# Up projection by seven products for eight, output projection by quarters of tokens, up results by way of DRAM

## The chip, the cores and the metric

One core of a Trainium2 chip runs the whole program. Its engines are TensorE (PE, with its weight loads PEld), VectorE (DVE), ScalarE (ACT), GpSimd (POOL) and SyncE (SP), from whose queue all DMAs of this kernel go out. The metric is the device time of one execution in microseconds, as the median of several runs.

## The reference

One inference step of a hybrid decoder layer in float32, for 1024 prompt tokens and 8 x 4 sample tokens (T = 1056 tokens in all), 1024 features. The part around the change:

```
hn  = rms_norm(x, norm_mix_pre)
mix = hybrid_mixer(hn, ...)        # three head groups, concatenated, then mix @ w_out  (1024 x 1024)
x   = x + rms_norm(mix, norm_mix_post)
hn  = rms_norm(x, norm_ffn_pre)
up  = hn @ w_up                    # 1024 x 5632: gate | val, 2816 features each
gate = causal_dwconv(gate)         # width 3; new state is an output
f   = (gelu(gate) * val) @ w_down  # 2816 x 1024
y   = x + rms_norm(f, norm_ffn_post)
```

## The kernel before

Activations lie with features on the 128 partitions and tokens along the free dimension. A product in float32 is made of three fp32r matmuls: each operand is split into a rounded part and the rest (`wh` and `wl` for weights, `xh` and `xl` for tokens), and `wh xh + wh xl + wl xh` is summed in one PSUM bank. `load_w` (L256) brings a weight tile of 128 outputs, up to 8 k of 128 x 128 (512 KB), by one DMA into the staging tile `w` (one buffer), casts it to `wh` on ACT (L264) and subtracts on POOL to `wl` (L265); `wh` and `wl` have two buffers each. `dense` (L268) runs the 3 x 8 matmuls of one output tile for one group of G = 352 tokens (three groups).

The order of PE's instructions in the mixer and the output projection is written out by `Weave` (L116): streams of work with ranks, each step yielding how long its next step has to wait by a virtual clock; what can't go yet is filled with dense work. Near its end the small products of the sample tokens (`samples`) are woven with the output projection. `project` (L1567) runs output tiles for groups 0 and 1 while the samples go on, then the rest and group 2, with further weight tiles and staging tiles (`places`, `stage`) cut out of memory that the mixer no longer needs. `finish` (L1620) normalises a group, adds the input, writes the sum to DRAM (`x1_dram`), and splits the next operands (L330). The factor per token of the second norm is not applied to the operands but to each product when it leaves PSUM (`scaled`, L296).

The ConvFFN (from L1655) goes through 22 tiles of hidden features in five parts. `gate_conv` (L1663) makes the gate tile for three groups, the convolution on ACT and DVE (L1682) and the gelu; `value` (L1687) the other tile, the product of both (L1695 to L1698), and its split into `hidh` and `hidl` (L1700, L1701), which stay in SBUF. After each part `down` (L1705) multiplies its hidden tiles with 8 output tiles of the down weights for three groups and adds into `fa` on DVE (L1734). In the last part `final` (L1746) of one group is laid between the products of the next; its steps are the sum of squares (L344), `rstd_of` (L305), two element-wise passes (L1754, L1755) and the output DMAs.

Of the kernel before, what the change touches and what calls it, by code (L numbers as in the profile page):

```python
# [8 lines left out]
F32 = mybir.dt.float32  # L9
# [14 lines left out]
KD = D // P  # L24
G = 352
NG = 3
NCH = SEQ // P
# [4 lines left out]
QUARTERS = ((0, 5), (5, 10), (10, 14), (14, 18), (18, 22))  # L32
# [3 lines left out]
# (kind, unit, tiles as (section, tile in the section, conv tile or None))  # L36
# [6 lines left out]
# the order of the dense work of the mixer  # L43
# [3 lines left out]
# columns of the packed vectors  # L47
# [9 lines left out]
# how far the urgent steps go ahead in the scheduler's order  # L57
FIRST = 1500
# how far apart two steps of one stream are set in the tensor engine's order, by what comes between them
# [5 lines left out]
    s_norm=6310, rows1=9000, rows2=6960, rows3=8500, f_rows=18400, f_0=5120, f_1=8920,  # L65
# [4 lines left out]
CUT = 4  # L70
# [8 lines left out]
LAST = 3  # L79

# columns of the packed constants
# [12 lines left out]
def constants():  # L94
# [5 lines left out]
    # what takes the place of NEG and LV for the samples  # L100
# [92 lines left out]
def kernel(ctx: ExitStack, tc: tile.TileContext, I, O):  # L193
# [31 lines left out]
    hnp = ctx.enter_context(tc.tile_pool(name="hnp", bufs=1))  # L225
    wp = ctx.enter_context(tc.tile_pool(name="wp", bufs=2))
    left, right = ExitStack(), ExitStack()
# [22 lines left out]
    x1_dram = drp.tile([NG, P, KD, G], F32, name="x1_dram")  # L250
# [32 lines left out]
    def hn_operand(k, g):  # L283
        return hh[g][:, k, :], hl[g][:, k, :]
# [1596 lines left out]
```

## Time and profile before

| | us |
|---|---|
| runs | 1575.71, 1578.13, 1581.62 (median 1578.13) |
| span of the profiled execution | 1578.6 |
| PE busy in it | 1496.2 |
| DVE busy | 920.7 |
| ACT busy | 542.1 |
| POOL busy | 546.1 |
| mean granted clock of PE | 0.977 |

The profiled execution has its span, from the first to the last instruction, and no other time of its own. A busy share is the union of an engine's instructions; matmuls are pipelined, so that one lasts longer than its distance from the next. The page cuts the span into slices; the views below cut it into stages: up to 652 us the mixer, then the samples with the output projection, the seam to the ConvFFN, the ConvFFN from 814.7 on, and what comes after its last product at 1558.2.

### The profile page before, as it was taken

The numbers are of one execution on the slowest core, as the hardware profiler recorded it, in microseconds if no ns is written. First come the engines' busy times: TensorE is split into PE (matmuls) and PEld (weight loads), VectorE is DVE, ScalarE is ACT, GpSimd is POOL, SyncE is SP. The second block draws the span as 40 slices with busy tenths as digits, with TensorE's granted clock in tenths as the row PEclk, the third lists the DMA queues.
The fourth block names the chain that finished last, engine by engine and source line by source line (L and its number), as shares of the span: only waits on it lengthen the run. The fifth ranks groups of instructions, "written<-read, shape, count | busy, mean of one in ns | idle before, by whom it ended". The sixth has DMA issues, their size and how long they took to land.

```text
span 1578.6 us, 24157 instructions
## 1 busy us (share of the span) xinstructions
PE 1496.2 (95%) x9438; PEld 1453.1 (92%) x9438; DVE 920.7 (58%) x1818; ACT 542.1 (34%) x1173; POOL 546.1 (35%) x624
## 2 busy tenths in 40 slices
PE   8788999989999999999899999999999999999995
PEld 8788899879989989988889999999999999999994
DVE  6889888796474367636975522444245325424558
ACT  7644445443342232424652211221122112212353
POOL 6234433232354353566432122221222222122224
PEclk9989999999999999999999999999999999999997
DMA  5111010111111231324531112111111111111142
GB/s 180 43 48 30 23 45 25 34 32 30 43 55 47 79 112 47 102 76 152 187 100 41 44 42 62 41 41 42 52 54 34 41 61 42 40 55 54 52 151 110
DMA packets 51210, 100.63 MB, mean 64 GB/s; under 512 B 14857, under 2 KB 25737, under 8 KB 50713
## 3 DMA queue, kind: packets, MB, share of 16 engines
q1 hardware_dynamic: 51096, 99.10, 20.1%
q8 instruction: 74, 1.21, 0.3%
q14 instruction: 40, 0.32, 0.1%
HBM read 85.25 MB, written 13.31 MB: 62 GB/s over the span
## 4 chain that ended last, share of the span: by engine, by line
PE 63%; DVE 17%; ACT 6%; POOL 5%; issue 4%; DMA 4%; SPq 0%; DVEq 0%; POOLq 0%; ACTq 0%
PE acc L203 55%; PE mc L203 3%; PE mb L203 3%; DVE kq L465 2%; PE mb L207 2%; DMA E<-rows_dram 2%; POOL wl L265 1%; DVE hl L333 1%; DVE two L784 1%; DVE v L465 1%; ACT sq L212 1%; POOL E L868 1%; PE po L203 1%; DVE fs L344 1%; ACT E L212 1%
## 5 line engine op out<-in xcount | busy, mean ns | idle before, releaser
L203 PE MATMUL acc<-hh,wh 128*128 128x352 f32 x1952 | 660.7, 339 | 18.2 <-DVE pre L303 12.2
L203 PE MATMUL acc<-hh,wl 128*128 128x352 f32 x1960 | 635.8, 324 | 2.6 <-POOL wl L265 2.0
L203 PE MATMUL acc<-hl,wh 128*128 128x352 f32 x1952 | 631.9, 324 | 0.7 <-DVE hl L333 0.7
L203 PEld LDWEIGHTS acc<-hh,wh 128*128 128x128 f32 x1952 | 371.7, 191 | 25.3 <-DVE pre L303 8.5
L265 POOL TENSOR_TENSOR wl<-w,wh 128x1024 fp32r<-128x1024 f32 (+2 forms) x117 | 252.9, 2162 | 362.3 <-ACT wh L264 354.8
L203 PEld LDWEIGHTS acc<-hh,wl 128*128 128x128 f32 x1960 | 372.4, 190 | 4.2 <-POOL wl L265 2.3
L203 PEld LDWEIGHTS acc<-hl,wh 128*128 128x128 f32 x1952 | 373.0, 191 | 3.1 <-DVE hl L333 1.7
L264 ACT CAST wh<-w 128x1024 fp32r<-128x1024 f32 (+2 forms) x117 | 109.9, 939 | 416.4 <-PE acc L203 400.3
L203 PE MATMUL acc<-hidh,wh 128*128 128x352 f32 x444 | 143.8, 324 | 0.0
L203 PE MATMUL acc<-hidh,wl 128*128 128x352 f32 x444 | 143.3, 323 | 0.0
L203 PE MATMUL acc<-hidl,wh 128*128 128x352 f32 x444 | 143.2, 322 | 0.0
L303 DVE TENSOR_TENSOR fpre<-acc,rs 128x352 f32<-128x352 f32 (+1 forms) x88 | 35.8, 430 | 137.5 <-PE acc L203 135.1
L1734 DVE TENSOR_TENSOR fa<-fa,acc 128x352 f32<-128x352 f32 x96 | 49.8, 519 | 106.3 <-PE acc L203 105.9
L1682 DVE SCALAR_TENSOR_TENSOR fy<-fpre,vec,fy 128x1072 f32<-128x1072 f32 x44 | 79.3, 1802 | 36.7 <-ACT fy L212 36.0
L203 PEld LDWEIGHTS acc<-hidh,wh 128*128 128x128 f32 x444 | 83.4, 188 | 0.0
L203 PEld LDWEIGHTS acc<-hidl,wh 128*128 128x128 f32 x444 | 83.4, 188 | 0.0
L203 PEld LDWEIGHTS acc<-hidh,wl 128*128 128x128 f32 x444 | 83.4, 188 | 0.0
L1701 DVE TENSOR_TENSOR hidl<-hid,hidh 128x352 fp32r<-128x352 f32 x66 | 52.7, 799 | 37.8 <-ACT hidh L1700 37.8
L1677 POOL COPY ffn_o<-fpre 128x2 f32<-128x2 f32 x22 | 4.1, 186 | 157.8 <-DVE fpre L303 157.8
L465 DVE SCALAR_TENSOR_TENSOR kq<-pre,cw,kq 128x352 f32<-128x352 f32 (+1 forms) x72 | 53.4, 748 | 7.7 <-ACT kq L212 7.2
L1700 ACT CAST hidh<-hid 128x352 fp32r<-128x352 f32 x66 | 31.9, 483 | 74.2 <-DVE hid L1695 49.9
L303 DVE TENSOR_TENSOR hid<-acc,rs 128x352 f32<-128x352 f32 x66 | 34.4, 521 | 38.1 <-PE acc L203 38.1
(552 smaller groups left out, 2238.7 us busy)
## 6 DMA issues: line engine op xcount, KB each, us to landing
w<-in_w_up_dram SPq DMA_DIRECT2D x44, 512.0 KB
w<-in_w_in_dram SPq DMA_DIRECT2D x30, 512.0 KB
E<-rows_dram SPq DMA_DIRECT2D x24, 256.0 KB
w<-in_w_dn_dram SPq DMA_DIRECT2D x21, 256.0 KB
w<-in_w_out_dram SPq DMA_DIRECT2D x10, 512.0 KB
w<-in_w_dn_dram SPq DMA_DIRECT2D x16, 320.0 KB
xr<-in_xT_dram SPq DMA_DIRECT2D x24, 176.0 KB
hh<-x_dram SPq DMA_DIRECT2D x3, 1408.0 KB
```

Source lines behind the costliest of these rows:

```text
L203: return nc.tensor.matmul(out, **kw)
L207: return nc.tensor.transpose(out, in_, identity)
L212: i = nc.scalar.activation(**kw)
L264: nc.scalar.copy(out=wh[:, ks], in_=w[:, ks])
L265: gtt(out=wl[:, ks], in0=w[:, ks], in1=wh[:, ks].bitcast(F32), op=ALU.subtract)
L303: vtt(out=out, in0=ps, in1=r, op=ALU.mult)
L333: stt(out=hl[g][:, k, :], in0=x, scalar=col(vcol + k), in1=hh[g][:, k, :].bitcast(F32), op0=ALU.mult, op1=ALU.subtract)
L465: stt(out=y[:, a:b], in0=pre[:, a + j:b + j], scalar=cw2[:, 4 * t + j:4 * t + j + 1], in1=y[:, a:b], op0=ALU.mult, op1=ALU.add)
L1682: stt(out=y[:, :LF], in0=pre[:, j:j + LF], scalar=col(V_FW + 3 * f + j), in1=y[:, :LF], op0=ALU.mult, op1=ALU.add)
L1700: nc.scalar.copy(out=hidh[:, groups[g]], in_=hid)
L1701: vtt(out=hidl[:, groups[g]], in0=hid, in1=hidh[:, groups[g]].bitcast(F32), op=ALU.subtract)
L1734: vtt(out=fa[:, g, m, :], in0=fa[:, g, m, :], in1=ps[:, :G], op=ALU.add)
```

## The change

Tokens are now also cut into four quarters of Q = 264.

*Up projection.* Output tiles are taken in pairs, features in two halves of 4 k, tokens in two units of two quarters. Each pair and unit is thus a 2 x 2 by 2 x 2 block product, done by Winograd's form of Strassen's method: seven block products of 4 k x 3 matmuls with 264 columns in place of eight. The combinations of tokens (`operands`) are made once per unit, those of weights (`weight_pieces`) once per pair and use, each then split into two parts. The seven products accumulate in three PSUM banks per unit; between products, DVE or ACT reads a bank, and the next product goes on summing into it. For this the operands must be normalised completely, so `finish` applies the second factor itself.

*Output projection.* Quarters 0 and 1 together, then 2, then 3, each with all 8 weight tiles loaded anew; the subtraction for odd tiles is on DVE. The places and stages set aside are gone. After quarter 3, `head` runs the first pair's gate products for unit 0.

*Up results.* The product of gelu and value goes in float32 to `hid_dram`, and is loaded, cast and subtracted again in the down projection, which now comes as a whole after the up projection, in six parts and by quarters. PE's written order now holds to the program's end; the mixed values are one tile instead of eight.

```diff
+Q = 264
+NQ = 4
+PLACES = ({6: 4, 5: 5, 7: 6, 4: 7, 1: 0, 2: 1, 3: 2}, {1: 3, 6: 8, 5: 9, 7: 10, 2: 11, 4: 12, 3: 13})
+HEAD = 1
-QUARTERS = ((0, 5), (5, 10), (10, 14), (14, 18), (18, 22))
+PARTS = ((0, 2), (2, 6), (6, 10), (10, 14), (14, 18), (18, 22))
...
-            gtt(out=wl[:, ks], in0=w[:, ks], in1=wh[:, ks].bitcast(F32), op=ALU.subtract)
+            tt(out=wl[:, ks], in0=w[:, ks], in1=wh[:, ks].bitcast(F32), op=ALU.subtract)
...
+        def product(m, w, q):
+            ps = yield from dense(accp, w, hn_operand, KS, q, Q)
+            act(out=mix[m][:, quarters[q]], in_=ps[:, :Q], func=AF.Copy, scale=col(V_NPOST + m))
+            act(out=sqs[q][:, m, :], in_=ps[:, :Q], func=AF.Square)
+        def project(qs):
...
+            for m in range(KD):
+                w = load_w(I["w_out"][m], KD, tt=vtt if m % 2 else gtt)
+                for q in qs:
+                    yield from product(m, w, q)
+            for q in qs:
+                xs[q] = on.tile([P, KD, Q], F32, name="x", bufs=2)
+                dma(out=xs[q], in_=I["xQ"][q])
+                weave.add(finish(q, WAIT["f_wait"]), 8)
+        def project_first():
+            yield from project((0, 1))
+            split_mix(2, 0)
+            yield from project((2,))
+            have.add("three")
+        def project_last():
+            split_mix(3, 2)
+            yield lambda: late
+            late.pop(0)()
+            yield from project((3,))
+            have.add("projected")
...
+        def finish(q, wait):
+            t = total(q)
+            yield wait
+            r = rstd_of(on.tile([P, Q], F32, name="rstd", bufs=2), [t])
+            x = xs[q]
+            for i in range(2):
+                ks = slice(KH * i, KH * i + KH)
+                m = mx[:, ks, quarters[q]]
+                vtt(out=m, in0=m, in1=bc(r, 1, KH), op=ALU.mult)
+                vtt(out=x[:, ks], in0=x[:, ks], in1=m, op=ALU.add)
+                act(out=sqs[q][:, ks], in_=x[:, ks], func=AF.Square)
+                dma(out=x1_dram[q, :, ks], in_=x[:, ks])
+            t = total(q)
+            for k in range(KD):
+                act(out=mix[k][:, quarters[q]], in_=x[:, k, :], func=AF.Copy, scale=col(V_FPRE + k))
+            yield WAIT["f_rows"]
+            r = rstd_of(on.tile([P, Q], F32, name="rstd", bufs=2), [t])
...
+            vtt(out=t1, in0=B[0][1], in1=B[0][0], op=ALU.subtract)
+            vtt(out=t2, in0=B[1][1], in1=t1, op=ALU.subtract)
+            split(6, t2)
+            split(5, t1)
+            vtt(out=B[0][1], in0=B[1][1], in1=B[0][1], op=ALU.subtract)
+            split(7, B[0][1])
+            vtt(out=t2, in0=B[1][0], in1=t2, op=ALU.subtract)
+            split(4, t2)
+            late.append(lambda: (split(1, B[0][0]), split(2, B[1][0], gtt)))
+            late.append(lambda: split(3, B[1][1], gtt))
...
+    QS = [(1, 0), (6, 1), (5, 2), (7, 1), (2, 0), (4, 1), (3, 2)]
...
+        def weight_pieces(srcs):
+            A = [[None, None], [None, None]]
+            w = wp.tile([P, KD, P], F32, name="w", bufs=1)
+            for i, j in ((0, 0), (1, 0), (1, 1), (0, 1)):
+                A[i][j] = w[:, KH * i:KH * i + KH] if j == 0 else fg.tile([P, KH, P], F32, name="wq", bufs=2)
+                dma(out=A[i][j], in_=srcs[i][:, KH * j:KH * j + KH])
...
+            yield weight_piece(A[0][0])
+            vtt(out=s1, in0=A[1][0], in1=A[1][1], op=ALU.add)
+            vtt(out=s2, in0=s1, in1=A[0][0], op=ALU.subtract)
+            yield weight_piece(s2)
+            yield weight_piece(s1)
+            vtt(out=A[1][0], in0=A[0][0], in1=A[1][0], op=ALU.subtract)
+            yield weight_piece(A[1][0])
+            yield weight_piece(A[0][1])
+            yield weight_piece(A[1][1])
+            vtt(out=s2, in0=A[0][1], in1=s2, op=ALU.subtract)
+            yield weight_piece(s2)
+        def fast(srcs, units, out):
+            banks, sb = {}, {}
+            for (p, b), (wh, wl) in zip(QS, weight_pieces(srcs)):
+                for u in units:
+                    first = p in (1, 6, 5)
...
+                    for k in range(KH):
+                        kw = dict(skip_group_check=not first)
+                        mm(ps, lhsT=wh[:, k, :], rhs=xh[:, k, :], start=first and k == 0, stop=False, **kw)
+                        mm(ps, lhsT=wh[:, k, :], rhs=xl[:, k, :], start=False, stop=False, **kw)
+                        mm(ps, lhsT=wl[:, k, :], rhs=xh[:, k, :], start=False, stop=k == KH - 1, **kw)
+                        yield 0
+                    if p == 1:
+                        sb[u, 1] = fg.tile([P, Q], F32, name="f1", bufs=2)
+                        nc.scalar.copy(out=sb[u, 1], in_=ps)
+                    elif p in (6, 7):
+                        sb[u, p] = fg.tile([P, Q], F32, name=f"f{p}", bufs=2 if p == 6 else 1)
+                        vtt(out=sb[u, p], in0=sb[u, 1], in1=ps, op=ALU.add)
+                        if p == 7:
+                            out(1, 1, u, sb[u, 7], banks[u, 2])
+                    elif p == 2:
+                        out(0, 0, u, None, ps)
+                    elif p == 4:
+                        out(1, 0, u, sb[u, 1], ps)
+                    elif p == 3:
+                        out(0, 1, u, sb[u, 6], ps)
...
+        def head():
+            yield lambda: "projected" in have
+            late.pop(0)()
+            for i in range(HEAD):
+                pres[i] = gate_pres()
+                yield from fast(w_pair(i, 0), (0,), gate_out(pres[i]))
...
+        gates(0)
+        for i in range(NF // 2):
+            if i + 1 < NF // 2:
+                gates(i + 1)
+            hids = [hid4[:, (2 * i + j) % 4, :] for j in range(2)]
+            drain(fast(w_pair(i, 1), range(2), value_out(ys.pop(i), hids)))
+            for j in range(2):
+                dma(out=hid_dram[2 * i + j], in_=hids[j])
...
+        for qi, (f0, f1) in enumerate(PARTS):
+            hid = []
+            for f in range(f0, f1):
+                x = fp.tile([P, T], F32, name="hx", bufs=2)
+                dma(out=x, in_=hid_dram[f])
+                h, l = (fp.tile([P, T], F32R, name=f"hid{y}{f - f0}", bufs=2) for y in "hl")
+                nc.scalar.copy(out=h, in_=x)
+                vtt(out=l, in0=x, in1=h.bitcast(F32), op=ALU.subtract)
+                hid.append((h, l))
```

## Rows read from the trace of the kernel before

**Rows 1.** The page's first part: busy us, share of the span, instructions of each engine.
```profile
PE 1496.2 (95%) x9438; PEld 1453.1 (92%) x9438; DVE 920.7 (58%) x1818; ACT 542.1 (34%) x1173; POOL 546.1 (35%) x624
```
**Rows 2.** Table by stretches: length, busy us of PE, PEld, DVE, ACT, POOL, clock, DMA.
```profile
652.00:706.00 54.00, 53.32 (x366) 47.42 (x367) 16.30 (x44) 16.45 (x40) 33.55 (x33) 1.00 0.22 77
706.00:760.00 54.00, 53.59 (x305) 48.66 (x304) 38.79 (x46) 26.42 (x52) 35.38 (x20) 1.00 0.50 159
760.00:814.70 54.70, 45.27 (x236) 41.98 (x235) 47.69 (x79) 32.34 (x67) 20.10 (x16) 0.91 0.47 148
814.70:1509.40 694.70, 694.69 (x4346) 694.69 (x4347) 296.27 (x444) 149.92 (x190) 165.38 (x164) 1.00 0.16 51
1509.40:1558.20 48.80, 47.73 (x292) 46.72 (x290) 33.34 (x57) 28.78 (x55) 17.45 (x14) 1.00 0.26 99
1558.20:1578.60 20.40, 2.71 (x4) 1.12 (x4) 16.08 (x24) 3.22 (x6) 9.54 (x9) 0.56 0.37 141
```
**Rows 3.** Chain of waits in order of time: start us, us, what; its longest piece.
```profile
814.71 694.66 PE acc L203 x4344
```
**Rows 4.** Timeline and groups by shape, PE and PEld: matmuls and weight loads of other sizes.
```profile
138.12 0.61 PE L203 MATMUL mb<-V,Gt 128*128 128x128 f32 x4
561.23 1.03 PE L203 MATMUL mb<-qm,kq 128*128 128x256 f32 x4
683.97 0.57 PEld L203 LDWEIGHTS mc<-kqG,hh 128*128 128x128 f32 x4
...
L203 PE MATMUL mb<-V,Gt 128*128 128x128 f32 x128 | 19.0, 275 | 0.0
L203 PE MATMUL mb<-qm,kq 128*128 128x256 f32 x32 | 8.3, 382 | 0.5 <-POOL qm L1088 0.5
L203 PEld LDWEIGHTS mc<-kqG,hh x32: 187/192/192, 681.8 to 691.1; 128*128 128x128 f32 x32
```
**Rows 5.** DMA issues of the output weights: out<-in, count, KB each.
```profile
w<-in_w_out_dram SPq DMA_DIRECT2D x10, 512.0 KB
...
v<-in_w_out_dram SPq DMA_DIRECT2D x5, 512.0 KB
```
**Rows 6.** Chain of waits, the seam: a step on DVE, a weight load's DMA.
```profile
768.25 0.43 DVE mix L1630
...
793.99 3.57 DMA w<-in_w_up_dram
```
**Rows 7.** Instructions on the tile `w`: duration ns min/median/max, first and last start.
```profile
L264 ACT CAST wh<-w x117: 603/1048/1068, 34.8 to 1521.7; 128x1024 fp32r<-128x1024 f32 x83, 128x512 fp32r<-128x512 f32 x18, 128x640 fp32r<-128x640 f32 x16
L265 POOL TENSOR_TENSOR wl<-w,wh x117: 1287/2389/3278, 36.5 to 1522.7; 128x1024 fp32r<-128x1024 f32 x83, 128x512 fp32r<-128x512 f32 x18, 128x640 fp32r<-128x640 f32 x16
...
L265 POOL TENSOR_TENSOR hl<-w,hl x2: 1288/1294/1301, 1509.9 to 1515.5; 128x512 fp32r<-128x512 f32 x2
```
**Rows 8.** Table by stretches of the instructions on `acc` alone (PE, PEld, DVE, ACT).
```profile
652.00:706.00 54.00, 36.82 (x165) 25.84 (x165) 0.00 (x0) 2.71 (x6) 1.00 0.22 77
...
814.70:1509.40 694.70, 694.69 (x4346) 694.69 (x4347) 119.08 (x249) 0.00 (x0) 1.00 0.16 51
1509.40:1558.20 48.80, 47.14 (x288) 46.10 (x286) 11.81 (x23) 0.00 (x0) 1.00 0.26 99
```
**Rows 9.** The page's costliest groups: a convolution step, count | busy, mean ns | idle before.
```profile
L1682 DVE SCALAR_TENSOR_TENSOR fy<-fpre,vec,fy 128x1072 f32<-128x1072 f32 x44 | 79.3, 1802 | 36.7 <-ACT fy L212 36.0
```
**Rows 10.** Instructions on the tile `acc`: an eviction on DVE, ns min/median/max.
```profile
L1734 DVE TENSOR_TENSOR fa<-fa,acc x96: 506/521/522, 1087.9 to 1563.4; 128x352 f32<-128x352 f32 x96
```
**Rows 11.** Timeline of the seam: two additions on DVE, and POOL at that time.
```profile
755.16 0.51 DVE L1630 TENSOR_TENSOR mix<-mix,xr 128x352 f32<-128x352 f32 x1
758.27 2.72 DVE L1630 TENSOR_TENSOR mix<-mix,xr 128x352 f32<-128x352 f32 x1
...
758.10 2.52 POOL L265 TENSOR_TENSOR wl<-v,wh 128x1024 fp32r<-128x1024 f32 x1
```
**Rows 12.** Chain of waits in the tail: the sums over the partitions.
```profile
1563.50 2.73 PE po L203 x4
```

More of the change, by code (lines that the diff above doesn't have):

```diff
@@ L1639 @@
-        on = right.enter_context(tc.tile_pool(name="on", bufs=1, side="right"))
-        ssum = [sums(on, f"ss{g}") for g in range(NG)]
-        with tc.tile_pool(name="smp", bufs=1) as smp:
-            samples(smp)
-            split_mix(0)
-            split_mix(1)
-            weave.add(project(smp), 9)
-            weave.run(lambda: "projected" in have)
-        order.close()
-        weave.run(lambda: not weave.streams)
-        drain(finish(2))
-    right.close()
+                xh, xl = hn_operand(k, q)
@@ new lines, in finish @@
+        def finish(q, wait):
[15 more added lines that the diff above has]
+            r = rstd_of(on.tile([P, Q], F32, name="rstd", bufs=2), [t])
+            if q >= 2:
+                yield lambda: "fx" in have
+            for i in range(2):
+                m = mx[:, KH * i:KH * i + KH, quarters[q]]
+                o = m if q < 2 else xnb[0][:, KH * i:KH * i + KH, Q * (q - 2):Q * (q - 1)]
+                vtt(out=o, in0=m, in1=bc(r, 1, KH), op=ALU.mult)
+            have.add(("normed", q))
+            if q == 1:
+                yield lambda: "fx" in have
+                operands(0, mx)
@@ L1651 @@
+        late = []
+        on = right.enter_context(tc.tile_pool(name="on", bufs=1, side="right"))
+        smp_done = lambda: all(x + " samples" in have for x in ("gdn", "ml", "ssd"))
+        with tc.tile_pool(name="smp", bufs=1) as smp:
+            log_tables()
+            samples(smp)
+            split_mix(0, 0)
+            split_mix(1, 2)
+            weave.add(project_first(), 9)
+            weave.run(lambda: "three" in have and smp_done())
     left.close()
+    LF = 1072
+    QS = [(1, 0), (6, 1), (5, 2), (7, 1), (2, 0), (4, 1), (3, 2)]
@@ new lines, with gates @@
+        fo = ph.enter_context(tc.tile_pool(name="fo", bufs=1, side="right"))
+        fpool[1] = fo
+        operands(1, xnb[0])
+        ffn_o = fo.tile([P, NF, 18], F32, name="ffn_o")
+        st_ffn = fo.tile([P, NF, 16], F32, name="st_ffn")
+        dma(out=st_ffn, in_=I["st_ffn"])
+        hid4 = fx.tile([P, KD, 2 * Q], F32, name="xnb").rearrange("p a b -> p (a b)").rearrange("p (f t) -> p f t", t=T)
+        ys = {}
+        def gates(i):
+            units = (1,) if i < HEAD else (0, 1)
+            if i >= HEAD:
+                pres[i] = gate_pres()
+            drain(fast(w_pair(i, 0), units, gate_out(pres[i])))
+            ys[i] = [fo.tile([P, 1080], F32, name="fy", bufs=4) for j in range(2)]
+            for j in range(2):
+                gate_conv(2 * i + j, pres[i][j], ys[i][j])
@@ new lines, with down, down_w, final @@
+        gates(0)
[4 more added lines that the diff above has]
+            drain(fast(w_pair(i, 1), range(2), value_out(ys.pop(i), hids)))
+            for j in range(2):
+                dma(out=hid_dram[2 * i + j], in_=hids[j])
+        dma(out=O["ffn"], in_=ffn_o)
+    low.close()
+    with tc.tile_pool(name="fp", bufs=1) as fp, tc.tile_pool(name="accd", bufs=5, space=PSUM) as accd:
+        ssum = [sums(fp, f"fs{g}", 1, Q) for g in range(NQ)]
+        fa = fp.tile([P, NQ, KD, Q], F32, name="fa")
+        count = [0] * NQ
+        def down(m, w, g, qi, hid):
+            nf = len(hid)
+            ps = drain(dense(accd, w, lambda k, g: [t[:, quarters[g]] for t in hid[k]], nf, g, Q))
+            if qi == 0:
+                nc.vector.tensor_copy(out=fa[:, g, m, :], in_=ps[:, :Q])
+            else:
+                vtt(out=fa[:, g, m, :], in0=fa[:, g, m, :], in1=ps[:, :Q], op=ALU.add)
+            if qi == len(PARTS) - 1:
+                if g == NQ - 1 and count[g] == KD - 1:
+                    ssum[g].append(fp.tile([P, Q], F32, name="sq1", bufs=2))
+                    act(out=ssum[g][1], in_=fa[:, g, m, :], func=AF.Square)
+                else:
+                    square_sum(fp, fa[:, g, m, :], ssum[g], count[g])
+                count[g] += 1
+        def down_w(qi, m, held=False):
+            f0, f1 = PARTS[qi]
+            nf = f1 - f0
+            off = (f0 * KD + m * nf) * P * P
+            raw = fp.tile([P, KH, P], F32, name="wd", bufs=3)[:, :nf]
+            parts = [fp.tile([P, KH, P], F32R, name=f"wd{y}{m}" if held else f"wd{y}", bufs=1 if held else 3)[:, :nf]
+                     for y in "hl"]
+            return load_w(I["w_dn"][off:off + nf * P * P].rearrange("(p k c) -> p k c", p=P, k=nf), nf, raw, parts)
+        def final(g):
+            x = fp.tile([P, KD, Q], F32, name="xf", bufs=2)
```

362 lines of the change are left out of this document (160 added, 202 removed).

## The prediction

> **What bounds the kernel now.** I read the busy line of the page first: TensorE (PE) is busy for 1496.2 of 1578.6 us, VectorE (DVE) for 920.7, the others for a third [rows 1]. Such an average hides the stages, so the second view is the table by stretches [rows 2]. From 814.7 to 1509.4 us, the ConvFFN, PE is busy in all of the 694.70 us at clock 1.00, while DVE has 296.27 and ScalarE (ACT) 149.92: there PE alone sets the time. In 706 to 760 PE is dense too. In 760 to 814.7, the seam between the output projection and the ConvFFN, it is busy 45.27 of 54.70 us at clock 0.91. After 1558.2 comes a tail of 20.4 us with almost no PE. The chain of waits says the same: one piece of 694.66 us with 4344 products on `acc` [rows 3], which is 159.9 ns for a matmul of 352 columns. At 2.4 GHz 352 columns take 146.7 ns, so 13.2 ns go to something else at each matmul.
>
> The profile's one execution has a span of 1578.6 us and gives no time around it; the median of the three runs shown is 1578.13, so the sum is made against the span and needs no correction.
>
> **Columns saved and matmuls added.** Up projection before: 44 tiles x 3 groups x 8 k x 3 = 3168 matmuls of 352. After: 22 pairs x 7 products x 4 k x 3 x 2 units = 3696 of 264. Down projection: 1584 of 352 become 2112 of 264; output projection: 576 become 768. So only the up projection loses columns (1.115 to 0.976 million, 58 us at 2.4 GHz); the other two keep them and pay the 13.2 ns oftener.
>
> What does a 264-column matmul take? No row has one. If the 13.2 ns are fixed: 110.0 + 13.2 = 123.2. If they grow with columns (159.9/352 each): 119.9. A stream of fp32 matmuls bounds it from below: four of 256 columns span 1.03 us with 0.382 for one, so 216 ns each, and its arithmetic at the two cycles a column that it shows is 213.3; an overhead of 2.7 ns would make 112.7 [rows 4]. From above: four weight loads of 128x128 ahead of matmuls of 8 columns span 0.57 us with 0.19 for one, so a new load starts every 127 ns; four matmuls of 128 columns come at (0.61 - 0.275)/3 = 112 [rows 4]. A matmul shorter than its weight load would wait, and 264 columns are near that point: 127 is the upper end. I take 121.6, between the two readings of the fp32r row itself, since it is the same kind of instruction.
>
> So: up 3696 x 0.1216 = 449.4 against 506.6 us, -57; down 256.8 against 253.3, +3.5; output projection 93.4 against 92.1, +1.3. By PE alone the change gives 52 us. The rest of the working is what it gives back.
>
> The Trainium skill, "TensorE: Matmul & The Clock Gate", section "Back-to-back issue gap", gives N/2.4 + 2.5 ns for a warm matmul, 112.5 ns at 264 columns, estimated from it. By it 352 columns would take 149.2; the row has 159.9, so the trace disagrees for this data type. By it the sum would be 52 us lower.
>
> **The output projection by quarters.** Before, each of 8 weight tiles is loaded about twice (15 loads [rows 5]), some of them by way of a second staging tile `v`, and serves two groups, then the third. After, all 8 are loaded three times, for quarters (0, 1), for 2 and for 3: 24 loads, all through the one staging tile `w`. The next load can't start before the cast and the subtraction have read it. One load costs 3.57 us of DMA [rows 6], a cast of 1.05 on ACT and a subtraction of 2.39 on POOL [rows 7]: 7.0 us. With the subtraction on DVE (odd tiles), 1024 elements at 1.16 us by the 0.43 that a 352-element step takes in DVE's queue [rows 6], it is 5.8. Mean 6.4. For one quarter a tile feeds PE 24 x 0.1216 = 2.9 us, so for quarters 2 and 3 PE waits for weights.
>
> When does it begin? In 652 to 706 PE is full with the samples' small products; 165 of its 366 matmuls [rows 2] are on `acc` [rows 8]. That stretch I leave as it is. About 24 products precede it, and some 25 more fit as fillers are shorter, so at 706 some 215 of 384 for quarters 0 and 1 are through; the other 170 take 21 us, to about 723 with 4 us gained by shorter fillers. From there 15 loads x 6.4 = 96 us, plus the last product's 3: 822. PE alone would have been through in 2 x 23.3 us more than 723, at 770; the loads cost 52 us, of which before paid part as its own seam. With PE under half busy its clock may go to 1.2 GHz, as its mean of 0.91 in 760 to 814.7 shows for a lesser idling; a tile then feeds PE 5.9 us, still below a load, so that costs nothing there. The bounds of the load: 5.8 each (all subtractions as quick as DVE's) to 7.6 (a 7.0 load behind one 0.6 us step in ACT's or DVE's queue), 813 to 840.
>
> Then quarter 3 must be normalised and split before unit 1 can start. On DVE, at 1.2 us for 1056 elements (three steps of 0.43, less two starts): a reduction of 2112 elements (2.3), two multiplications and two additions (4.8), a second reduction (2.3), two multiplications (2.4), then in `operands(1)` t1, t2, three splits, two more combinations, a fourth split and only then the split for product 1, which PE wants first (9 steps, 10.8): 22.6, plus two rstd's of about 1.6 (a product, Ln, Exp): 25.8. `head` puts 84 products of unit 0 beneath it (10.2 us), which would otherwise come behind. So the ConvFFN is dense from about 847 instead of 814.7. Before, 4752 - 4346 - 288 = 118 of its matmuls were done by then [rows 8]; after, 84.
>
> **The dense stretch.** 3612 + 2112 = 5724 matmuls x 0.1216 = 696 us. What it adds beside PE, for a gate and a value pair (41 us of PE): POOL 14 pieces x 1.29 = 18 us [rows 7]; ACT about 15; DVE 8 weight sums (0.6), four conv steps of 1.8 [rows 9], some 32 evictions of 264 columns (0.52 for 352 [rows 10], less 0.09 for 88 columns: 0.43, and 0.34 apart), about 24 us. POOL and DVE hinder each other: at 758.27 a DVE addition took 2.72 us beneath a POOL subtraction of 2.52, one shortly before it 0.51 [rows 11]. With POOL busy 44% of the time some 8 us come to DVE's 24: 32 of 41. It has room, but product 7 may not enter its bank before DVE has read product 6 from it, which gives DVE 2.9 to 4.4 us with conv steps in its queue. Bounds: nothing (the deadline always met) to 1.5 us a pair, 33. I take 3 us. The operands' and results' PSUM banks (two and five) suffice by count.
>
> Up results go to DRAM and come back: 22 x 540 KB each way, against a DMA share of 0.16 in that stretch [rows 2]; hidden. Their cast and subtraction (about 2.4 us a tile) lie under 11.7 us of PE a tile. At the border the first down weights sit where the last up weights were, so PE waits for a small DMA, cast and subtraction: 5 us; at least 2, at most 12 if the first hidden tiles wait as well.
>
> **The tail.** Eviction, sum, products `po` (2.73 us at the lower clock [rows 12]), Ln, Exp and 16 steps on DVE and POOL go from 352 to 264 columns: 20.4 becomes about 17; bounds 15 and 20.4.
>
> **Sum.** 847 + 696 + 8 + 17 = 1568 us, 10 under the span: the dense stretch is 47 shorter (743.5 to 696) and the tail 3; the seam gives back 32, stalls and border 8.
>
> **Rivals.**
> *The seam hides the loads* (0.2): loads at 5.8, finishing under `head`, scheduler putting product 1's split early; the dense stretch starts near 815. 815 + 696 + 8 + 17 = 1536. For it: DVE is idle in much of 706 to 760 [rows 2]. Against it: one staging tile makes the chain serial whatever engines are free.
> *The overhead is that of the fp32 rows* (0.05): 112.7 ns a matmul, 5724 x 0.0089 = 51 less, 1517. For it: the 256-column row. Against it: 13.2 ns in every stretch of the ConvFFN. The gap that the Trainium skill gives, 112.5, is the same case.
> *DVE becomes the bound in the up projection* (0.18): the bank wait between products 6 and 7, decided where DVE's queue holds over 2.9 us. At 1.5 us a pair 30 more, 1598, slower. For it: the 2.72 us lock. Against it: evictions read PSUM, and of 96 none took over 0.522 us, POOL busy or not [rows 10].
> *264 columns are bound by the weight load* (0.12): 127 ns instead of 121.6, 5724 x 0.0054 = 31: 1599, slower, and with it all of the three projections pay. For it: the 127 ns stream. Against: 112 at 128 columns.
> The forecast itself holds 0.45, between 1550 and 1586.
>
> **How the numbers follow.** This kernel's measurement tells about 0.5% from no change: 1570 to 1586 is "same". Of the forecast's 0.45 some 0.27 lie below 1570 and 0.18 inside. Faster: 0.27 + 0.2 + 0.05 = 0.52; same 0.18; slower 0.18 + 0.12 = 0.30. The range leaves out 1517 below with the fringe of 1536, and above the case that both slow ones strike together: 1530 to 1606.
>
> **What would show it.** Matmuls in the ConvFFN about 121.6 ns apart (112 or 127 speak for rivals); between some 723 and 822 PE half idle on `wl`, with the load queue waiting for the subtractions; a PE gap of 10 to 20 us before unit 1's first product; in the up stretch PE idle under 1% and, if not, released by DVE's addition for product 6. The forecast is wrong if the dense stretch starts before 830 or after 865, or if DVE's waits come to over 15 us.

## The result and the profile after

The changed kernel takes 1682.37 us (median of four runs, 1680.14 to 1687.18) against 1579.46 for the kernel before (1575.71 to 1581.62): a ratio of 1.066, 95% interval 1.064 to 1.068. The forecast was 1568, with a range up to 1606. The profiled execution has a span of 1685.4 us, so 117 us have to be found against the sum.

First the page's busy line, beside [rows 1]: PE is busy as long as before, to 0.4 us, so the other 106 us of the longer span are idle time of PE. But the forecast took 52 us off PE's busy time. That it did not fall goes with the mean granted clock, 0.938 here and 0.977 before: a matmul at the lower clock counts as busy for longer, as the 24 that take 4.68 us below show.

```profile
PE 1496.6 (89%) x10692; PEld 1446.3 (86%) x10692; DVE 1057.7 (63%) x2039; ACT 631.7 (37%) x1380; POOL 667.6 (40%) x737
```

The table by stretches of the changed kernel, with the columns of [rows 2], follows. Its first rows do not end with the stages: the last product of quarters 0 and 1 ends near 725, that of quarter 2 at 803.4, that of quarter 3 near 871. Normalisation lasts to 917; then come the up projection to 1394, the border, the down projection and the tail. The last row is 100 us from inside the down projection.

```profile
706.00:740.00 34.00, 24.42 (x163) 21.18 (x162) 24.39 (x36) 14.51 (x39) 7.87 (x6) 0.91 0.26 89
740.00:760.00 20.00, 8.57 (x33) 6.45 (x31) 18.14 (x13) 13.11 (x26) 1.41 (x2) 0.56 0.51 190
760.00:820.00 60.00, 38.28 (x202) 32.83 (x200) 32.24 (x25) 21.34 (x36) 12.64 (x6) 0.80 0.34 115
820.00:860.00 40.00, 24.27 (x108) 22.03 (x109) 10.18 (x7) 14.17 (x27) 7.04 (x3) 0.70 0.25 86
860.00:917.00 57.00, 27.61 (x140) 25.38 (x139) 44.11 (x29) 24.37 (x41) 30.65 (x18) 0.71 0.20 69
...
945.00:1394.00 449.00, 430.62 (x3407) 428.80 (x3408) 277.90 (x453) 145.05 (x238) 220.68 (x216) 0.97 0.21 71
1394.00:1405.00 11.00, 0.55 (x5) 0.34 (x3) 2.66 (x5) 2.65 (x4) 0.07 (x1) 0.75 0.70 262
1405.00:1666.00 261.00, 260.24 (x2117) 259.62 (x2118) 127.59 (x256) 75.11 (x129) 74.77 (x62) 0.99 0.34 108
1666.00:1686.00 20.00, 2.49 (x8) 1.23 (x6) 13.26 (x27) 4.65 (x10) 7.41 (x9) 0.58 0.30 109
...
1500.00:1600.00 100.00, 100.00 (x825) 100.00 (x824) 39.77 (x77) 20.15 (x28) 25.22 (x19) 1.00 0.27 81
```

The last row gives the matmul of 264 columns: 100.00 / 825 = 121.2 ns. The forecast took 121.6. The rest of the table says where the 117 us are:

| | forecast | in the trace | |
|---|---|---|---|
| end of quarter 3's products | 822 | 871 | +49 |
| then to the dense ConvFFN | 25 | 46 (to 917) | +21 |
| up and down projection, with border and stalls | 704 | 749 (to 1666) | +45 |
| tail | 17 | 19 | +2 |

*Quarters 2 and 3.* The chain of waits of the changed kernel in quarter 3 (start us, us, what), two weight tiles:

```profile
840.71 5.22 PE acc L209 x22
...
846.33 0.38 ACT sq L218
846.71 0.94 ACT wh L273
...
847.68 1.24 DVE wl L274
...
854.30 0.38 ACT sq L218
854.68 0.94 ACT wh L273
...
855.69 2.35 POOL wl L274
...
858.09 5.22 PE acc L209 x22
```

Product (5.2 us, at clock 0.70), the square that empties its bank, the cast of the next tile, its subtraction: one after the other, 17.4 us for two tiles. No DMA stands in this piece. The cast waits for nothing but its place in ACT's queue, behind two evictions which wait for the product. At clock 1.00 a product takes 2.92 us, so, by this chain, some 2.3 us of a tile's 8.7 go with the low clock.

Quarter 2 loses more: its products run from some 725 to 803.4, 79 us where the forecast had 51 (8 x 6.4), and quarter 3's take 67 where it had 48; the start is 2 late. In quarter 2 the load's DMA does stand in the chain, with 3.3 to 4.0 us, and DVE comes on top. The cast of the second tile is done at 726.07, but its subtraction starts on DVE at 750.90. In between, DVE has the last splits of the mixed values, three of the reductions and eight steps of the normalisation of quarters 0 and 1, of which the last five stand here:

```profile
725.02 1.05 ACT L273 CAST wh<-w 128x1024 fp32r<-128x1024 f32 x1
```

```profile
742.39 2.42 DVE L1625 TENSOR_TENSOR mix<-mix,rstd 128x1056 f32<-128x1056 f32 x2
744.73 3.92 DVE L1614 TENSOR_REDUCE ss<-sq 128x264 f32<-128x2112 f32 x1
748.56 2.42 DVE L1626 TENSOR_TENSOR x<-x,mix 128x1056 f32<-128x1056 f32 x2
750.90 1.22 DVE L274 TENSOR_TENSOR wl<-w,wh 128x1024 fp32r<-128x1024 f32 x1
```

PE's waits in 706 to 872 (us in total, times, longest) name the cast, the subtractions, and also the reductions `ss`: PE's written order lays the products `po` of the normalisation of quarters 0 and 1 between the products of quarter 2.

```profile
PE acc L209 <- ACT wh L273: 22.1, 13, 2.8
PE acc L209 <- DVE wl L274: 16.5, 8, 11.2
PE acc L209 <- POOL wl L274: 12.3, 6, 2.7
PE po L209 <- DVE ss L1614: 8.2, 2, 5.0
```

*Normalisation.* Behind each quarter stand two reductions of 2112 elements, and the unit's operands. The group on the tile `ss` (duration ns min/median/max) and the chain:

```profile
L1614 DVE TENSOR_REDUCE ss<-sq x8: 3912/4024/4067, 728.3 to 892.7; 128x264 f32<-128x2112 f32 x8
```
```profile
901.59 2.32 DVE xnb L1639
...
905.57 2.25 DVE fy L1668
...
907.85 3.37 DVE fy L1669
911.22 2.29 DVE xnb L1672
913.51 2.34 POOL fpre L1801 x2
```

Each reduction takes 4.0 us where the forecast had 2.3, and most of the operands' 1056-element steps between 899 and 916 take some 2.2 to 3.5, where it had 1.2. POOL is busy up to 915.9, with pieces of weights and two of the operands' splits; a step of this size at 916.88 takes 1.24 again. That POOL is the cause fits [rows 11], but no run tested it. The forecast also left out the products of `head` beside these steps: DVE runs 13 steps for them in 870 to 906, 10.8 us, and the product `po` of the first reduction, done at 876.42, stands behind them in PE's order, so that its result is used only at 883.53.

*Up projection.* From 945 to 1394 there are 3407 matmuls; at 121.2 ns they are 413 of 449 us, so 36 are lost. The chain repeats the same piece every 44.46 us:

```profile
1132.08 2.94 PE accr L209 x24
...
1135.07 1.82 issue
1136.89 2.37 DVE fy L1806
1139.26 0.35 DVE f L1762
...
1139.75 4.68 PE accr L209 x24
```

PE starts no matmul for 2.1 us (the list of waits counts 1.8), until DVE's sum `f` of product 6 is there, and the 24 matmuls after it take 4.68 instead of 2.92 us. The timeline of DVE shows what stands ahead of the sum, four convolution steps without a gap; the list of PE's waits in 960 to 1380 (us in total, times, longest) has this one wait and no other:

```profile
1132.11 7.15 DVE L1806 SCALAR_TENSOR_TENSOR fy<-fpre,vec,fy 128x1072 f32<-128x1072 f32 x4 [1.43 <-ACT fy L218]
1139.18 0.76 DVE L1762 TENSOR_TENSOR f<-f,accr 128x264 f32<-128x264 f32 x2
```
```profile
PE accr L209 <- DVE f L1762: 18.1, 10, 1.8
```

The granted clock is 1.00 from 1132 to 1137.6, 0.64 in the mean of the stretch behind the gap, and 1.00 again from 1144.5 to 1170. Of the 24 matmuls 15 come 0.22 us apart, at the level of 1.2 GHz, the others 0.12:

```profile
1139.70:1144.50 4.80, 4.75 (x26) 4.79 (x27) 3.42 (x4) 1.72 (x3) 2.98 (x2) 0.64 0.30 96
```

Ten such gaps, at 2.1 us and 1.8 of slower matmuls, make 39, about the 36 lost. The rest of the +45 is the border, some 5 us in 917 to 945, and 4 in the down projection.

*Border.* 10.7 us without products: the last store to DRAM, the first load behind it in SP's queue, then cast and subtraction.

```profile
1395.43 2.67 DMA hid_dram<-xnb
...
1398.61 4.79 DMA hx<-hid_dram
...
1403.42 1.07 ACT hidh L1925
1404.49 0.32 ACT wdh L273
...
1404.93 1.44 POOL wdl L274
```

### The profile page after: what moved, and what is told of

Its sections match the earlier page's. It is cut to its first block, busy times and chain, and to the rows that moved or that the text cites. A ratio compares the mean times of both kernels' runs of the same rounds, so it can differ in the third digit from the quotient of the medians.

```text
span 1685.4 us, 27745 instructions
## 1 busy us (share of the span) xinstructions
PE 1496.6 (89%) x10692; PEld 1446.3 (86%) x10692; DVE 1057.7 (63%) x2039; ACT 631.7 (37%) x1380; POOL 667.6 (40%) x737
## 4 chain that ended last, share of the span: by engine, by line
PE 60%; DVE 18%; ACT 7%; issue 6%; POOL 5%; DMA 4%; SPq 0%; DVEq 0%; POOLq 0%; ACTq 0%
PE acc L209 35%; PE accr L209 17%; PE mb L209 3%; PE mc L209 3%; DVE fy L1806 2%; DVE kq L477 2%; POOL wl L274 2%; DMA E<-rows_dram 2%; PE mb L213 1%; ACT wh L273 1%; DVE two L796 1%; DVE v L477 1%; POOL E L880 1%; DVE fa L1913 1%; PE po L209 1%
## 5 line engine op out<-in xcount | busy, mean ns | idle before, releaser
L209 PE MATMUL acc<-hh,wh 128*128 128x352 f32 (+1 forms) x1344 | 451.6, 336 | 37.2 <-ACT wh L273 22.1
L209 PE MATMUL acc<-hh,wl 128*128 128x352 f32 (+1 forms) x1352 | 428.5, 317 | 29.9 <-DVE wl L274 16.5
L209 PE MATMUL acc<-hl,wh 128*128 128x352 f32 (+1 forms) x1344 | 423.3, 315 | 0.1
L209 PE MATMUL accr<-hh,wh 128*128 128x264 f32 x880 | 261.2, 297 | 41.7 <-DVE f L1762 24.5
L209 PE MATMUL accr<-hl,wh 128*128 128x264 f32 x880 | 259.8, 295 | 4.0 <-DVE hl L1659 4.0
L209 PE MATMUL accr<-hh,wl 128*128 128x264 f32 x880 | 259.0, 294 | 0.5 <-POOL wl L1715 0.5
L209 PEld LDWEIGHTS accr<-hh,wh 128*128 128x128 f32 x880 | 175.0, 199 | 44.8 <-issue 24.8
L209 PE MATMUL acc<-hidh,wdh 128*128 128x264 f32 x704 | 201.5, 286 | 10.4 <-ACT wdh L273 10.4
L209 PE MATMUL acc<-hidh,wdl 128*128 128x264 f32 x704 | 201.1, 286 | 0.8 <-POOL wdl L274 0.8
L209 PE MATMUL acc<-hidl,wdh 128*128 128x264 f32 x704 | 200.7, 285 | 0.0
L209 PEld LDWEIGHTS acc<-hidh,wdh 128*128 128x128 f32 x704 | 133.4, 190 | 10.8 <-ACT wdh L273 10.7
```

The costliest lines, as they stand in the source:

```text
L209: return nc.tensor.matmul(out, **kw)
```

## The experiments

Theory A: quarters 2 and 3 are slow through the place of the cast in ACT's queue. Theory B: the up stretch is slow through the convolution ahead of the sums in DVE's queue. The rivals stand in the expectations. All runs, each against the kernel before on the same chip; one per cent is 15.8 us, and the changed kernel is at 1.066.

| run | edit, beside the changed kernel | us | ratio to before (95%) |
|---|---|---|---|
| e1 | second staging buffer | 1637.5 | 1.039 (1.037 to 1.040) |
| e2 | sums ahead of the convolution | 1661.4 | 1.054 (1.052 to 1.056) |
| e3 | quarters 2 and 3 together | 1640.2 | 1.041 (1.039 to 1.042) |
| e4 | 14 loads left out | 1615.5 | 1.025 (1.023 to 1.026) |
| e5 | 24 idle matmuls a product | 1681.7 | 1.068 (1.064 to 1.071) |
| e6 | e1 + e2 | 1627.2 | 1.032 (1.029 to 1.036) |
| e7 | e6 + shorter normalisation | 1615.4 | 1.025 (1.022 to 1.028) |
| e8 | e7 + e3 | 1612.3 | 1.022 (1.019 to 1.025) |
| e9 | 12 idle matmuls a product | 1664.0 | 1.056 (1.054 to 1.058) |
| e10 | banks read by ACT | 1666.4 | 1.057 (1.055 to 1.059) |
| e11 | e3 + e7's shorter normalisation + e10, two pairs in `head`, border loads from ACT's queue | 1603.6 | 1.018 (1.016 to 1.019) |
| e12 | cast ahead of the evictions, subtraction earlier too | 1665.2 | 1.056 (1.053 to 1.060) |
| e13 | no convolution on DVE | 1650.6 | 1.048 (1.043 to 1.052) |
| e14 | e11, but quarters 0 to 2, then 3 with its casts ahead | 1618.1 | 1.028 (1.025 to 1.031) |

**e1, e3, e4: the loads.**

```diff
-            w = wp.tile([P, kk, P], F32, name="w", bufs=1)
+            w = wp.tile([P, kk, P], F32, name="w", bufs=2)      # e1, three places
```


> The changed kernel with two buffers instead of one for the staging tile of the weights. Theory A (in quarters 2 and 3 of the output projection the cast of the next weight tile stands in ScalarE's queue behind the copy and the square of the running product, so that product, evictions, cast and subtraction come one after the other, 8.7 us a tile, with TensorE at half clock): the cast can now be queued before the evictions; a tile falls to 5 to 6 us, 15 tiles give 45 to 55 us, and the time is about 1632 (1615 to 1645). Rival B (the chain DMA, cast, subtraction of one tile, 3.6 + 1.0 + 1.2 or 2.4 us, is the bound, and a second buffer only lays the DMA beside the rest): a tile still takes 6.4 to 7 us, 1650. Rival C (what holds the quarters back is the squares' buffer and the normalisation steps on VectorE): no change, 1675 to 1688.


```diff
             yield from project((0, 1))                           # e3
-            split_mix(2, 0)
-            yield from project((2,))
...
+            split_mix(2, 0)
             split_mix(3, 2)
+            yield from project((2, 3))
...
-            yield from project((3,))
```


> The changed kernel with quarters 2 and 3 projected together as 0 and 1 are: 16 loads of output weights instead of 24. Theory A (each load costs TensorE its whole cycle of 8.7 us): eight tiles with 5.8 us of products at full clock each, plus evictions, cast and subtraction behind them, 9 to 10 us a tile, 75 to 80 us instead of about 149; quarter 2 is normalised later, beside quarter 3, which gives back 10 to 20. Time about 1630 (1610 to 1645). Rival C (normalisation on VectorE is the bound of the whole seam): 1665 to 1690, since all of it now comes behind the last product.


```diff
-                w = load_w(I["w_out"][m], KD, tt=vtt if m % 2 else gtt)
+                if m == 0 or qs[0] < 2:                          # e4
+                    w = load_w(I["w_out"][m], KD, tt=vtt if m % 2 else gtt)
```


> The changed kernel with quarters 2 and 3 of the output projection using the first weight tile for all eight output tiles: 14 of the 24 loads are left out, and their casts and subtractions (the product is another one). It bounds what the reloading costs altogether. Theory A: the 16 products run at 2.9 to 3.5 us each, 46 to 56 us instead of about 149 with the gap ahead of quarter 2, and the time falls by 75 to 100 us, to about 1595. Rival C (the squares' buffer and VectorE's normalisation hold the quarters back whatever the weights do): less than 40 us, above 1642.

e1 gives 2.7%, 43 us, inside A's window; e3 2.5%, 40 us, as A had it (rival C, that normalisation alone is the bound, falls); e4 4.1%, 65 us, under A's 75 to 100. So the 14 loads that e4 leaves out cost 65 us in all; the rest of the seam's loss has other causes, which e4 does not part. With the loads out of the way PE meets the next queue: in 700 to 960 its longest total wait is for the reductions `ss`, 22.0 us in e1 and 27.6 in e3, where it was 8.2 before them; and the wait of 11 us for quarter 2's second subtraction is still there in e1.

**e5, e9, e12: clock or queue.** That PE's half clock "costs nothing there" is a claim of the forecast, and the chain above seems to speak against it, since the 5.2 us are in it. e5 and e9 keep PE busy with matmuls that nothing reads; e12 puts the cast of the next tile ahead of the evictions on ACT. It issues the next load earlier for that, and so DVE's subtraction moves forward too.

```diff
+        for _ in range(idle):                                    # e5, e9
+            nc.tensor.matmul(ps[:, :P], lhsT=ones, rhs=ones, start=True, stop=True)
...
-            ps = yield from dense(accp, w, hn_operand, KS, q, Q)
+            ps = yield from dense(accp, w, hn_operand, KS, q, Q, 24 if q >= 2 else 0)   # e9: 12
```


> The changed kernel with 24 small matmuls of 128 columns, which nothing reads, on the bank of each product of quarters 2 and 3 ahead of it, where TensorE otherwise waits for the next weight tile (added work, nothing else changed). It tests the sentence 'half clock costs nothing there'. If TensorE's half clock is in the cycle (product 5.2 us instead of 2.9, then evictions, cast, subtraction, one after the other), the granted clock rises to 1.00 in quarters 2 and 3, a product takes 2.9 us, a tile 6.4 to 7 instead of 8.7, and 15 tiles give 25 to 35 us: about 1652. If the loads set the cycle whatever the clock, the time stays at 1675 to 1690, or rises by what the added matmuls take.

> As the run with 24 added matmuls ahead of each product of quarters 2 and 3, but with 12: there 24 took 5.2 us, so TensorE was full with them (8.3 us a tile) and nothing could be gained; 12 take 2.6 us, less than the 3.5 us that TensorE waits. If half clock is in the cycle: granted clock near 1.00, a product 2.9 us, a tile 6.2 to 7, 20 to 35 us less than 1682: 1647 to 1662. If the loads set the cycle whatever the clock: 8.3 to 8.7 us a tile and 1675 to 1690.


```diff
+            if after is not None:                                # e12, of several edits
+                in_order(ev, after)
...
+                    nxt = load_w(I["w_out"][m + 1], KD, tt=gtt if m % 2 else vtt)
```


> The changed kernel with one edge more in ScalarE's order for quarters 2 and 3: the cast of the next weight tile goes ahead of the evictions of the running product. One staging buffer as before, no added matmuls, so TensorE's clock may stay low. It parts what the runs with added matmuls mixed, since there the clock rose and the casts came ahead of the evictions too. If the place of the cast is the cause and half clock costs nothing, the chain of the load sets 6.2 to 6.5 us a tile, as with 12 added matmuls, and the time is about 1660 (1652 to 1667). If half clock is in the cycle, a tile takes 7.5 us or more: 1670 to 1682.

e5 parts nothing: its 24 added matmuls took 5.5 us a product, so PE was full, 8.3 us a tile at clock 1.00; its time lies at the rival's number, but with PE full that says nothing of either. e9 raised the clock and gave 1.0%, 16 us, just short of its window; but in its order the casts had come ahead of the evictions too. e12 moves the cast and leaves the clock as it comes. The table of 800 to 840 us of e9, then of e12:

```profile
800.00:840.00 40.00, 38.04 (x315) 37.00 (x314) 16.72 (x12) 18.61 (x35) 7.55 (x3) 1.00 0.31 108
```
```profile
800.00:840.00 40.00, 27.20 (x148) 24.45 (x148) 15.46 (x11) 17.97 (x34) 7.09 (x3) 0.83 0.31 106
```

Clock 1.00 in the one, 0.83 in the other, and the same time (1.056 both). e12's ACT shows the casts now released by the DMA, not by PE; four tiles, from 812.38 to 838.45, take 6.5 us each:

```profile
819.19 1.04 ACT L275 CAST wh<-w 128x1024 fp32r<-128x1024 f32 x1 [5.12 <-DMA w<-in_w_out_dram]
...
825.84 1.05 ACT L275 CAST wh<-w 128x1024 fp32r<-128x1024 f32 x1 [4.94 <-DMA w<-in_w_out_dram]
826.96 0.48 ACT L218 ACTIVATE mix<-acc,vec 128x264 f32<-128x264 f32 x1
```

Once the cast is ahead, then, the lower clock costs nothing: the chain DMA, cast, subtraction sets 6.5 us, as the forecast's 6.4 had it. With the cast behind the evictions the product is in series with the load, and the 2.3 us of the low clock count. By the same chain, an estimate: at full clock its tile would take 8.7 less 2.3, some 6.4 us, too. A raised clock alone might so have done as much; no run shows it, as in e5 and e9 the casts moved as well.

Nor is e12's gain the cast's alone. About half of it lies in quarter 2, whose products end at 789.2 in place of 803.4; there the subtraction that had stood at 750.90 now comes 25 us earlier, ahead of DVE's normalisation, and PE's wait of 11.2 us is gone. The other half lies in quarter 3, 52 us in place of 63.

```profile
725.76 1.22 DVE L276 TENSOR_TENSOR wl<-w,wh 128x1024 fp32r<-128x1024 f32 x1
```

**e2, e10, e13: the up stretch.**

```diff
+                        with tc.high_priority(offset=FIRST):     # e2
                             vtt(out=sb[u, p], in0=sb[u, 1], in1=ps, op=ALU.add)
```


> The changed kernel with the sum that frees the bank of product 6 (and that of product 7) put ahead of the convolution's steps in VectorE's queue; nothing else is moved by hand. Theory (the 2.1 us gap of TensorE at every gate pair comes from four convolution steps in a row ahead of this sum, and the clock falls after it, 3.7 us a pair in all): ten to twenty such gaps go, the time falls by 25 to 40 us to about 1648, and a stretch of 44.5 us with 336 matmuls becomes one of 41. Rival (the sum is late because the locking of VectorE and GpSimd stretches whatever stands in its queue): the gaps only move to other releasers, 1675 to 1688.


```diff
-                        vtt(out=sb[u, p], in0=sb[u, 1], in1=ps, op=ALU.add)   # e10
+                        nc.scalar.copy(out=sb[u, p], in_=ps)
+                        vtt(out=sb[u, p], in0=sb[u, 1], in1=sb[u, p], op=ALU.add)
```


> The changed kernel with the banks of products 6 and 7 read by a copy on ScalarE, and the sum made on VectorE from that copy: the bank no longer waits for VectorE's queue, and the convolution's place in it is as it was. If that queue is the whole cause of the up stretch's loss, the 2.1 us gaps go without any reordering and 30 to 38 us with them: about 1648. If VectorE is behind in any case (the sums late there hold up the results of products 4 and 3), new waits of TensorE for VectorE's additions take their place: above 1665.


```diff
-            for j in (1, 0):                                     # e13
+            for j in ():
```


> The changed kernel without the convolution's two steps on VectorE for each gate tile (a third of the convolution alone is left; the result is another). If these steps ahead of the sums for products 6 and 7 are the whole cause of the up stretch's loss, the gaps and the half clock after them go, and the time falls by 32 to 40 us to about 1646. If VectorE is late for another reason (the locking with GpSimd), gaps remain and the fall is under 20 us.

e13 gives 1.8%, 29 us: a little under its window, and PE's waits for the sum in 960 to 1380 fall from 18.1 us to those of three gaps (first line below). The convolution's steps are the cause of most of the 36 us. e2 gives 1.2%, 19 us, less than foreseen: three steps still stand ahead of the sums. e10 gives 0.9%, 14 us, near the rival's number, but by another wait: PE now waits for ACT's copy, which in its turn stands behind the gelu, which waits for the same steps on DVE (the other two lines, ACT of e10).

```profile
PE accr L209 <- DVE f L1762: 4.6, 3, 1.8
```
```profile
1167.13 1.10 ACT L218 ACTIVATE fy<-fy 128x1072 f32<-128x1072 f32 x1 [1.90 <-DVE fy L1807]
1168.14 0.36 ACT L1762 COPY f<-accr 128x264 f32<-128x264 f32 x1
```

**e6, e7, e8: together, and the normalisation.**

> The second staging buffer and the sum ahead of the convolution together. Alone they took 45 and 21 us from 1682. If they are two places that don't touch (the output projection, the up projection), the sum holds: 1616 (1612 to 1621). If part of the one gain is the other's (VectorE is freer in both), less: 1625 to 1637.


```diff
-            act(out=sqs[q][:, m, :], in_=ps[:, :Q], func=AF.Square)   # e7, of several edits
...
+            act(out=sq, in_=ps[:, :Q], func=AF.Square)
+            if m:
+                vtt(out=sqs[q], in0=sqs[q], in1=sq, op=ALU.add)
...
-            r = rstd_of(on.tile([P, Q], F32, name="rstd", bufs=2), [t])
+            r = rstd_of(on.tile([P, Q], F32, name="rstd", bufs=2), [mix[k][:, quarters[q]] for k in range(KD)])
```


> The kernel of the run before with a shorter normalisation chain: each square is added to a sum of 264 columns as it comes, in place of one reduction of 2112 elements (3.8 to 4.1 us on VectorE); the second sum of squares is made by eight ones-products on TensorE; the norm's weight and factor go on in one step per feature tile; and of unit 1's operands product 1's is split first, product 5's on GpSimd. Theory D (what is left of the seam is VectorE's chain of reductions and splits behind each quarter, 45 us from quarter 3's last product to unit 1's first dense stretch, of which two reductions are 8 and the place of product 1's split is 10): 15 to 25 us less than the run before, about 1596. Rival (TensorE finds other waits in that stretch at the same time, above all the next weight pieces, and the loads): less than 6 us.

> The kernel of the run before, with quarters 2 and 3 projected together (16 loads instead of 24). If the loads still cost TensorE after the second buffer, 8 fewer of them give 10 to 20 us: about 1580. If the normalisation of quarter 2, which now comes behind the last product instead of beside quarter 3, costs as much, it is the same within 6 us or slower.

e6 is 8 us short of the sum of e1 and e2; why, no run shows. e7 takes 0.7% off e6, 11 us, where 15 to 25 were expected: PE's wait for unit 1's operands ends 16 us earlier than in e6, and part of that went to waits behind it. e8's 0.3% is not told apart from e7, as the intervals overlap: with a second buffer, the number of loads hardly matters any more.

**e11, e14: what the change can be worth.**

```diff
+HEAD = 2                                                         # e11, of several edits
+                (nc.scalar.dma_start if qi == 0 else dma)(out=x, in_=hid_dram[f])
```


> All mends in one, to see what the change can be worth: quarters 2 and 3 together, the shorter normalisation chain, products 6 and 7 read by ScalarE, two pairs of gates of unit 0 instead of one beneath the normalisation of the last quarters, and the first hidden tiles of the down projection loaded from another queue than the stores of the last; one staging buffer, for the room. By the parts: 1612 (the run with the shorter chain and 16 loads) less 10 to 15 in the up stretch, 10 for the second pair, 3 to 5 at the border, and 5 to 8 more for the single staging buffer: about 1592, still not below the kernel before (1577). It would be below only if the dense stretch started by 840.


```diff
-            yield from project((0, 1))                           # e14, of several edits
+            yield from project((0, 1, 2))
```


> The kernel with all mends, but quarters 0, 1 and 2 projected together and then 3 (16 loads too), the casts of quarter 3's weights ahead of the evictions, so that quarters 0 to 2 are normalised beneath quarter 3's loads and only quarter 3's normalisation stands behind the last product. Quarters 0 to 2 need 2.9 x 3 = 8.7 us of TensorE a tile, more than a load of 6.3, and end at about 755; quarter 3 takes 8 x 6.3 = 50, to 805; then one normalisation and unit 1's operands, 40 us with 20 us of gate products beneath: dense from about 845, where the kernel with all mends was so from about 895. If theory A and D are right: 30 to 50 us less than 1604, 1555 to 1575, at or below the kernel before. Rival (VectorE's queue, with three normalisations and unit 0's operands beside quarter 3, holds up that quarter's loads and evictions): 1585 or more.

e11 has neither e1's second buffer nor e2. It is the best, 1603.6, 12 above what its parts were to give, and still 1.8% slower than before. In its up stretch PE is full, at 200.00 / 1645 = 121.6 ns:

```profile
1000.00:1200.00 200.00, 200.00 (x1645) 200.00 (x1645) 137.06 (x211) 83.02 (x156) 106.64 (x109) 1.00 0.22 80
```

There the seven products earn all that was reckoned, and the seam still takes more. At the border PE still waits 9.7 us, now for the DMA of the first down weights: loading the hidden tiles from another queue did not shorten it. e14 fell to its rival: 16 us slower than e11. PE's waits in 690 to 950 name a subtraction on DVE, which stood behind the normalisation and the operands of the first three quarters:

```profile
PE acc L209 <- DVE wl L276: 15.4, 2, 14.7
```

So moving this quarter only moved the place where DVE's work is met. What is left of the seam in e11 is not one engine's: PE's waits in 690 to 950 sum to some 47 us and name ACT, DVE and POOL (about 21, 15 and 11), and no run parts them. No version made here beats the kernel before.

## Why the prediction was wrong, by its steps

**Right: the products.** 121.6 ns against 121.2; down projection 261 us against 256.8; the weight load does not bound them. The gap that the Trainium skill states ("TensorE: Matmul & The Clock Gate", "Back-to-back issue gap") gives 112.5 ns, an estimate from it; the trace disagrees at 264 columns as it did at 352.

**Wrong: "From there 15 loads x 6.4 = 96 us, plus the last product's 3: 822"**, +49. The load's chain was sized well (e12: 6.5). What failed is that nothing but that chain was counted: cast and subtraction were priced at their durations, 1.05 and 1.16 to 2.39, and not at their places in the queues of ACT and DVE. In quarter 3 (+19) the cast stands behind evictions that wait for PE. In quarter 2 (+28) the second tile's subtraction also stands 24.8 us behind DVE's splits and normalisation of quarters 0 and 1, and PE's `po` products behind their reductions; this normalisation stood in the sum with nothing. Against the changed kernel e12 gives back 15 us with earlier places on ACT and DVE, e1 43 with a second buffer. How the 28 divide between DVE's queue and the cast's place, no run shows; e14 meets a wait of the same kind at 14.7.

"So that costs nothing there", said of the half clock, holds where the cast is ahead (e12), and not in the kernel as it stood: the forecast compared the tile's 5.9 us with the load's 6.4 as if they ran side by side, and in quarter 3 they ran in series.

The Trainium skill, "Perfetto Trace Analysis", section "Tensor Engine Instruction (MATMUL, LD_WEIGHTS)", says that ScalarE, VectorE and GpSimd work strictly in order. The trace agrees, with the cast at 846.71.

**Wrong: the normalisation, "25.8"**, +21: the reduction was sized by elements of an addition (2.3; 4.0 measured), and steps of 1.2 us took up to 3.5. The products of `head` were counted as free beneath it; their 10.8 us of steps on DVE and their place in PE's order were put at nothing. Product 1's split did not come last either, as the sum had it: it was done early, and PE, at product 6, then waited 12.8 us for ACT's cast and 4.0 for DVE's split, till 917. e7 took back 11.

**Wrong: "I take 3 us" for the stalls of the up stretch**, +33. The deadline was named rightly, "with conv steps in its queue", and the rival "DVE becomes the bound" had the size (30). But the four steps were counted as load on a queue with room, 32 of 41 us, instead of as one block of 7.15 us against a deadline of 2.9 to 4.4. And each late sum costs twice: 2.1 us of waiting and 1.8 of slower matmuls after it. e13 shows 29 of the 36.

**Border and tail:** 10.7 instead of 5, inside its bounds of 2 to 12; 19 instead of 17, as the last `xf` load came late, behind the `out_y` stores by the chain; no run tested this.

The bound of 1606 held DVE's stalls and slow matmuls together; a seam 70 us late was in no case. The seam's forecast and its rival (847 and 815) both assumed that a load's engines are free when its data comes. For it the rival named a DVE "idle in much of 706 to 760"; [rows 2] have it busy for 38.79 of the 54 us. Both of the forecast's own signs of being wrong came: the ConvFFN is dense from 917, later than 865, and DVE's waits in the up stretch are 18.1 us and not under 15.

## What to carry to other kernels

Price a step that feeds TensorE by its place in its engine's queue: list what stands ahead of it, and what those wait for. If that is the product it is to overlap, the stage is serial. Here a second staging buffer gave 43 us, and earlier places for cast and subtraction 15. A queue that is 78% busy can miss a deadline shorter than its longest run of steps: compare the block, not the share. And a cheaper algorithm that needs complete operands moves normalisation onto the critical path: here the 57 us earned in products were outweighed by the seam, where reloading weights alone cost 65 (e4).

## What was not expected of the hardware

After a gap of 2.1 us PE's next 24 matmuls took 4.68 us instead of 2.92, at a granted clock of 0.64 in 1139.70 to 1144.50. A reduction over a strided axis took 4.0 us for 2112 elements, 1.9 ns each, where an addition of 1056 (L1626, two in 2.42) takes 1.2 us, 1.1 each; that the stride is the cause is not tested. A float32 matmul of 128 columns among others of its kind takes 0.23 us (24 in 5.5 us, in e5), nearly twice one of 264 columns in fp32r.
